# Weight sums moved from GpSimd to VectorE, and low halves of feed-forward weights formed by an accumulating DMA

## The chip, the cores and the metric

The kernel runs on one core of a Trainium2 chip. The time is device time of one launch in microseconds, the median of several runs. A profile is one execution, taken by the hardware profiler; its span runs from the first to the last instruction. In its rows PE is TensorE's matmul, PEld its weight load, DVE VectorE, ACT ScalarE, POOL GpSimd, and SP the engine that issues most DMAs. L12 is line 12 of the kernel.

## The reference

Two layers of an encoder for 512 positions of 1024 channels, in float32. Cut to what matters here:

```python
def reference(x, norm1_g, w_in, ..., w_out, norm2_g, w_ffn_in, w_ffn_out):
    for l in range(DEPTH):
        h = rmsnorm(x, norm1_g[l])
        ...    # differential attention, convolution branch, Fourier branch, gates
        x = x + merged @ w_out[l]
        h2 = rmsnorm(x, norm2_g[l])
        f_gate, f_up = jnp.split(h2 @ w_ffn_in[l], 2, axis=-1)
        x = x + (jax.nn.silu(f_gate) * f_up) @ w_ffn_out[l]
    return x
```

The feed-forward block is 2816 wide, which is 22 blocks of 128.

## The kernel before, in words

**Two halves of each number.** A float32 operand is used as a high half (a copy rounded to the float32r format, made on ScalarE) and a low half (the operand minus that copy, on VectorE). A product is then three matmuls: high by high, high by low and low by high. Everything is held with channels on the partitions and the 512 positions along the row.

**Weights in chunks.** The host lays all weights out as chunks of eight 128x128 blocks in the order of use. `chunk` loads one (512 KB, tile `raw`, shown as `wr`), lets ScalarE make `hi` (L201, tile `wh`) and VectorE `lo` (L202, tile `wl`). The pools hold WB = (3, 4, 4) buffers of `raw`, `hi` and `lo`. `gemm` uses the chunk block by block (L121).

**The feed-forward block.** It is done in two halves of eleven units; a half ends with eight outputs of the second projection (`gemm(act)`, L547 adds each to the residual), for which eleven chunks are loaded. A unit makes one block of the gate and one of the up projection in seven block products instead of eight (the scheme of Strassen and Winograd). `pair_weights` loads two chunks, `r1` with the blocks a21 and a11 and `r2` with a22 and a12, each 128x512, and forms

- s1 = a21 + a22 (L260), s3 = a11 - a21 written over a21 (L261), s2 = s1 - a11 (L263), s4 = a12 - s2 (L266), all on GpSimd;
- high and low halves of both loaded chunks, of which the first now holds s3 and a11 (L251 on ScalarE, L252 on VectorE, 128x1024 each);
- high and low halves of s1, s2 and s4 (L154 on ScalarE, L155 on VectorE, tiles `A` or `att`).

`combine` forms the matching sums of the input on VectorE (L295 to L298) while the attention output is being projected. `pair_gemm` runs the seven products (L281): four go into two banks of PSUM, then ScalarE copies the first bank (L328), VectorE adds the second (L329, tile `p15`), and TensorE adds three further products into the same banks, the last of them into the bank that L329 has read. `unit` then combines the banks on VectorE (L521 to L529), with a SiLU on ScalarE (L524), and splits the result for the second projection.

**What sets the order.** Nothing is in a hand-written order. Each instruction gets a priority, a due time that `self.t` counts up by the matmuls' lengths; the weights of a pair are asked for WLS = 20000 ns ahead, those of a chunk WL = 16000. A scheduler plays the program through with these priorities at build time and writes a fixed order for every engine; at run time each engine goes through its order and waits where an operand or a buffer isn't there yet. SP issues all weight loads, in order. GpSimd also adds squares for the norms (L353) and merges the branches (L574).

Of the kernel before, what the change touches and what calls it, by code (L numbers as in the profile page):

```python
# [9 lines left out]
F32 = mybir.dt.float32  # L10
F32R = mybir.dt.float32r
I32 = mybir.dt.int32  # L12
AF = mybir.ActivationFunctionType
ALU = mybir.AluOpType
AX = mybir.AxisListType

P = 128
L = 2
D = 1024
T = 512  # L20
# [9 lines left out]
CHUNK = 8  # L30
# [27 lines left out]
PEORD = False  # L58
CONV_LOW = -20000
WL = 16000  # L60
WB = (3, 4, 4)
WLS = 20000
HALF = 108
PASS = 216
MAGIC = 0x5F3759DF
# [23 lines left out]
class Hybrid:  # L89
# [102 lines left out]
    def chunk(self, l, c, t):  # L192
        nc = self.nc
        tc = self.tc
        keep = tc.cur_priority
        self.at(t - WL)
        raw = self.wp.tile([P, CHUNK * P], F32, tag="raw", name=self.nm("wr"), bufs=WB[0])
        nc.sync.dma_start(raw, self.a["w"][l, c])
        hi = self.wp.tile([P, CHUNK * P], F32R, tag="hi", name=self.nm("wh"), bufs=WB[1])
        lo = self.wp.tile([P, CHUNK * P], F32R, tag="lo", name=self.nm("wl"), bufs=WB[2])  # L200
        nc.scalar.copy(hi, raw)  # L201
        nc.vector.tensor_tensor(out=lo, in0=raw, in1=hi.bitcast(F32), op=ALU.subtract)  # L202
        tc.cur_priority = keep
        return hi, lo

# [23 lines left out]
    def pair_weights(self, early):  # L229
        nc, tc = self.nc, self.tc  # L230
        keep = tc.cur_priority
        self.at(self.t - WLS)
        raws = []
        for _ in range(2):
            raw = self.wp.tile([P, CHUNK * P], F32, tag="raw", name=self.nm("wr"), bufs=WB[0])
            c, k = divmod(self.wi, CHUNK)
            assert k == 0
            nc.sync.dma_start(raw, self.a["w"][self.l, c])
            self.wi += CHUNK
            raws.append(raw)  # L240
        r1, r2 = raws
        a21, a11 = r1[:, 0:T], r1[:, T : 2 * T]
        a22, a12 = r2[:, 0:T], r2[:, T : 2 * T]
        tags = ("qst", "kst", "ar") if early else ("cv", "cv", "cv")
        s1, s2, s4 = (self.slot(tag) for tag in tags)
        out = {}

        def halves(names, src):
            hi = self.wp.tile([P, CHUNK * P], F32R, tag="hi", name=self.nm("wh"), bufs=WB[1])
            lo = self.wp.tile([P, CHUNK * P], F32R, tag="lo", name=self.nm("wl"), bufs=WB[2])  # L250
            nc.scalar.copy(hi, src)  # L251
            nc.vector.tensor_tensor(out=lo, in0=src, in1=hi.bitcast(F32), op=ALU.subtract)  # L252
            for i, n in enumerate(names):
                out[n] = (hi[:, i * T : (i + 1) * T], lo[:, i * T : (i + 1) * T])

        def single(name, src):
            out[name] = self.split_to(src, "att" if early else "A")

        g = nc.gpsimd.tensor_tensor
        g(out=s1, in0=a21, in1=a22, op=ALU.add)  # L260
        g(out=a21, in0=a11, in1=a21, op=ALU.subtract)  # L261
        halves(("s3", "a11"), r1)
        g(out=s2, in0=s1, in1=a11, op=ALU.subtract)  # L263
        single("s1", s1)
        single("s2", s2)
        g(out=s4, in0=a12, in1=s2, op=ALU.subtract)  # L266
        halves(("a22", "a12"), r2)
        single("s4", s4)
        tc.cur_priority = keep
        return out  # L270

    def product(self, ps, w, xs, ks, start, stop):
        wh, wl = w
# [190 lines left out]
    def main(self, l):  # L464
        nc = self.nc
        sm = self.small
        hb = sm(24, "hb")
        nc.vector.tensor_scalar_mul(hb, self.par(l, "bg"), 0.5)
        hcw = sm(4 * CW, "hcw")
        nc.vector.tensor_scalar_mul(hcw, self.par(l, "cw"), 0.5)  # L470
        self.hb, self.hcw = hb, hcw
        self.glu(l)
        if l == 0:
            self.tables()
        self.qkv(l)
        self.heads(l, self.t + ATT0, ATT)
        self.four_c(l)
        merged = self.merged
        ths = []
        for m in range(KT):  # L480
            pg = self.gemm(self.h)
            ths.append(self.tanh(pg, 0, m, "A"))
        thb = [self.tanh(self.gemm(self.h), 1, m, "M") for m in range(LEAD_B)]
        self.drain("conv")
        for m in range(KT):
            py = self.gemm(self.cvs)
            self.merge(m, thb.pop(0), py)
            if m + LEAD_B < KT:
                thb.append(self.tanh(self.gemm(self.h), 1, m + LEAD_B, "M"))
        self.drain("att")  # L490
        ms = []
        for m in range(KT):
            py = self.gemm(self.atts)
            self.merge(m, ths[m], py)
            ms.append(self.split_to(merged[m], "cv" if m < 4 else "A"))
        x2, xc, acc = [None] * KT, [], None
        g2 = self.par(l, "g2")
        h = T // 2
        for q in range(KT // 2):
            us = self.wtp.tile([P, 2, T], F32, tag="wth", name=self.nm("us"))  # L500
            ts = self.wtp.tile([P, 2, T], F32, tag="wtl", name=self.nm("ts"))
            for i, m in enumerate((q, q + KT // 2)):
                xr = self.slot("M")
                self.at(self.t - 20000)
                getattr(nc, QS[3]).dma_start(xr, self.xin[m])
                self.at(self.t)
                ps = self.gemm(ms)
                xt = self.slot("V")
                nc.vector.scalar_tensor_tensor(out=xt, in0=ps, scalar=0.5, in1=xr, op0=ALU.mult, op1=ALU.add)
                nc.scalar.activation(us[:, i, :], xt, AF.Copy, scale=g2[:, m : m + 1])  # L510
                acc = self.sq_add(xt, acc, "M")
                x2[m] = xt
            xc.append(self.combine(us[:, 0, :], us[:, 1, :], (ts[:, 0, :], ts[:, 1, :]), XCT[q]))
        self.xg, self.acc = [], None
        xin = []
        rb2 = None

        def unit(j, b1, b2, qw):
            z = self.slot("M")
            v = nc.vector.tensor_tensor  # L520
            v(out=z[:, 0:h], in0=b1[:, 0:h], in1=rb2[:, 0:h], op=ALU.mult)  # L521
            v(out=z[:, h:T], in0=b1[:, h:T], in1=qw[:, 0:h], op=ALU.add)
            v(out=z[:, h:T], in0=z[:, h:T], in1=rb2[:, h:T], op=ALU.mult)  # L523
            nc.scalar.activation(z, z, AF.Silu)  # L524
            u = self.slot("M")
            v(out=u[:, 0:h], in0=b2[:, h:T], in1=qw[:, 0:h], op=ALU.add)
            v(out=u[:, h:T], in0=qw[:, 0:h], in1=qw[:, h:T], op=ALU.add)
            v(out=u, in0=u, in1=rb2, op=ALU.mult)
            v(out=u, in0=u, in1=z, op=ALU.mult)  # L529
            if j < 4:  # L530
                t = self.wtp.tile([P, 2, T], F32R, tag="wth" if j < 2 else "wtl", name=self.nm("act"))
                return self.split(u, t[:, 0, :], t[:, 1, :])
            if j < 7:
                return self.split_to(u, "qst", "kst")
            return self.split_to(u, "att")

        for half in range(2):
            act = []
            for j in range(NJ // 2):
                w = self.pair_weights(half == 0 and j < 4)  # L540
                got = self.pair_gemm(j, w, xc, half == 0 and j == 0)
                if half == 0 and j == 0:
                    rb2 = self.inv_rms(acc, D, "M", "rb")
                act.append(unit(j, *got))
            for m in range(KT):
                ps = self.gemm(act)
                nc.vector.tensor_tensor(out=x2[m], in0=ps, in1=x2[m], op=ALU.add)  # L547
                if half == 0:
                    continue
                if l == L - 1:  # L550
                    nc.sync.dma_start(self.out[m], x2[m])
                else:
                    sc = self.dram.tile([P, T], F32, tag=f"x{l}_{m}", name=f"x{l}_{m}")
                    getattr(nc, QS[3]).dma_start(sc, x2[m])
                    xin.append(sc)
                    self.next_x(l + 1, m, x2[m])
        self.xin = xin
        self.x = x2
# [630 lines left out]
```

## Time and profile before

| | |
|---|---|
| median of 3 runs | 1706.0 us (1704.88 to 1706.34) |
| profiled execution | 1702.3 us, span 1700.2 us |
| mean granted TensorE clock | 0.975 |
| TensorE matmul busy | 1625.8 us, 96% |
| VectorE busy | 1426.2 us, 84% |
| ScalarE busy | 791.7 us, 47% |
| GpSimd busy | 411.8 us, 24% |
| moved by DMA | 178.77 MB, mean 105 GB/s |

The halves of the feed-forward block lie, for the first layer, at about 460 to 655 and 655 to 855 us of the span, and for the second at about 1300 to 1500 and 1500 to 1700. In each, the units come first and the eight outputs of the second projection after them. A busy share of the whole span is an average over stages with different limits; the stages have to be read one by one.

### The profile page before, as it was taken

The page shows a single profiled execution, that of the slowest core. Times are in us where ns is not written, and L with a number is a line of the kernel's source. Part 1 is how long each engine was busy: PE and PEld are TensorE (multiplying, and loading weights), DVE is VectorE, ACT ScalarE, POOL GpSimd, SP SyncE. Part 2 cuts the span into 40 slices and gives each one's busy share as a digit, 9 for nine tenths or more (in the row PEclk, how much of TensorE's full clock was granted, in tenths as well). Part 3 has the DMA queues.
Part 4 walks back from the last instruction along what each step waited for, and adds up shares of the span by engine and source line. Part 5 has one row for each costly group of instructions (what it writes and reads, how often), then busy time and mean ns, then how long its engine had stood idle before and what let it go on. Part 6 is the DMA issues. An engine that isn't in the chain of part 4 may idle for free.

```text
span 1700.2 us, 24154 instructions
## 1 busy us (share of the span) xinstructions
PE 1625.8 (96%) x9096; PEld 1419.3 (83%) x9096; DVE 1426.2 (84%) x2220; ACT 791.7 (47%) x1267; POOL 411.8 (24%) x261
## 2 busy tenths in 40 slices
PE   8999999999987999889999999998999889998899
PEld 6888888887787988889888888886887889888897
DVE  7999999897999946997469999997779999379962
ACT  6445545753554423444343455557435544234430
POOL 3000000114455405551200000001145553065500
PEclk8999999999988999999999999999999899999999
DMA  5554234222422332223442532332234223332241
GB/s 198 167 162 143 75 101 125 81 84 82 129 76 87 100 100 87 88 87 106 137 136 88 186 121 90 105 102 68 79 98 123 74 87 100 99 93 82 87 124 50
DMA packets 61460, 178.77 MB, mean 105 GB/s; under 512 B 8976, under 2 KB 9872, under 8 KB 61344
## 3 DMA queue, kind: packets, MB, share of 16 engines
q1 hardware_dynamic: 60912, 176.11, 33.8%
q8 instruction: 71, 1.16, 0.3%
q0 software_dynamic: 432, 1.13, 0.3%
q14 instruction: 45, 0.37, 0.1%
HBM read 163.30 MB, written 13.89 MB: 104 GB/s over the span
## 4 chain that ended last, share of the span: by engine, by line
PE 75%; DVE 17%; issue 4%; ACT 2%; DMA 1%; POOL 1%; SPq 0%; DVEq 0%; POOLq 0%; ACTq 0%
PE main L121 51%; PE s L281 5%; PE att L281 4%; PE s L121 4%; PE att L121 3%; DVE M L529 3%; PE main L281 3%; DVE wl L252 3%; PE oth L121 3%; DVE A L155 3%; PE att L131 2%; DVE att L155 1%; DVE M L329 1%; DMA wr<-in_w 1%; DVE M L523 1%
## 5 line engine op out<-in xcount | busy, mean ns | idle before, releaser
L201 ACT CAST wh<-wr 128x1024 fp32r<-128x1024 f32 x180 | 188.9, 1051 | 281.3 <-PE main L121 153.1
L202 DVE TENSOR_TENSOR wl<-wr,wh 128x1024 fp32r<-128x1024 f32 x180 | 233.0, 1295 | 74.6 <-ACT wh L201 73.9
L121 PE MATMUL main<-X,wh 128*128 128x512 f32 x864 | 277.4, 395 | 0.0
L121 PEld LDWEIGHTS main<-X,wh 128*128 128x128 f32 x864 | 161.4, 189 | 32.8 <-issue 0.5
L988 DVE SCALAR_TENSOR_TENSOR cv<-cv,hcw,cv 128x497 f32<-128x497 f32 (+14 forms) x240 | 176.6, 736 | 1.2
L121 PE MATMUL main<-X,wl 128*128 128x512 f32 x432 | 170.9, 396 | 0.0
L251 ACT CAST wh<-wr 128x1024 fp32r<-128x1024 f32 x88 | 92.4, 1050 | 116.5 <-PE att L281 29.4
L252 DVE TENSOR_TENSOR wl<-wr,wh 128x1024 fp32r<-128x1024 f32 x88 | 141.2, 1605 | 5.5 <-ACT wh L251 5.4
L1019 POOL TENSOR_TENSOR cv<-cv,cv 128x512 f32<-128x512 f32 x6 | 9.8, 1630 | 515.6 <-DVE cv L988 515.6
L260 POOL TENSOR_TENSOR cv<-wr,wr 128x512 f32<-128x512 f32 x36 | 53.4, 1485 | 298.0 <-DMA wr<-in_w 254.9
L121 PE MATMUL main<-att,wh 128*128 128x512 f32 x384 | 119.4, 390 | 1.5 <-ACT att L154 1.5
L155 DVE TENSOR_TENSOR A<-cv,A 128x512 fp32r<-128x512 f32 x108 | 108.7, 1008 | 13.2 <-ACT A L154 12.9
L812 ACT ACTIVATE at<-s,mx 128x512 f32<-128x512 f32 x128 | 88.1, 689 | 58.3 <-DVE mx L810 51.8
L121 PE MATMUL main<-A,wh 128*128 128x512 f32 x320 | 106.4, 391 | 0.0
L121 PE MATMUL main<-wh,X 128*128 128x512 f32 x288 | 96.7, 391 | 0.0
L154 ACT CAST A<-cv 128x512 fp32r<-128x512 f32 x108 | 65.4, 617 | 65.8 <-PE s L281 22.9
L121 PEld LDWEIGHTS main<-X,wl 128*128 128x128 f32 x432 | 81.6, 189 | 17.1 <-issue 0.5
L810 DVE TENSOR_REDUCE mx<-s 128x1 f32<-128x512 f32 x128 | 86.7, 681 | 3.8 <-PE s L121 3.1
L547 DVE TENSOR_TENSOR V<-main,V 128x512 f32<-128x512 f32 x32 | 22.1, 690 | 77.5 <-PE main L121 77.5
L121 PEld LDWEIGHTS main<-att,wh 128*128 128x128 f32 x384 | 71.8, 188 | 17.2 <-ACT att L154 1.7
L121 PE MATMUL main<-cv,wh 128*128 128x512 f32 x240 | 78.4, 395 | 2.9 <-ACT cv L154 2.8
L121 PE MATMUL main<-act,wh 128*128 128x512 f32 x256 | 80.2, 394 | 0.0
(324 smaller groups left out, 4399.2 us busy)
## 6 DMA issues: line engine op xcount, KB each, us to landing
wr<-in_w SPq DMA_DIRECT2D x268, 512.0 KB, 3.6
dqk<-at SPq DMA_DIRECT2D x32, 256.0 KB, 3.7
qst<-dqk SPq DMA_DIRECT2D x96, 64.0 KB, 1.9
kst<-dqk SPq DMA_DIRECT2D x96, 64.0 KB, 1.9
V<-in_xT SPq DMA_DIRECT2D x8, 256.0 KB, 7.0
att<-dftd SPq DMA_DIRECT2D x8, 256.0 KB, 4.5
M<-in_xT SPq DMA_DIRECT2D x8, 256.0 KB, 3.5
x<-V SPq DMA_DIRECT2D x8, 256.0 KB, 2.6
```

The lines of the kernel that those rows point to most:

```text
L121: return self.pin(self.nc.tensor.matmul(out, lhsT=lhsT, rhs=rhs, start=start, stop=stop))
L154: self.lasthi = nc.scalar.copy(hi, src)
L155: nc.vector.tensor_tensor(out=lo, in0=src, in1=hi.bitcast(F32), op=ALU.subtract)
L201: nc.scalar.copy(hi, raw)
L202: nc.vector.tensor_tensor(out=lo, in0=raw, in1=hi.bitcast(F32), op=ALU.subtract)
L251: nc.scalar.copy(hi, src)
L252: nc.vector.tensor_tensor(out=lo, in0=src, in1=hi.bitcast(F32), op=ALU.subtract)
L260: g(out=s1, in0=a21, in1=a22, op=ALU.add)
L281: self.nc.tensor.matmul(ps, lhsT=a[:, s], rhs=b, start=start and k == ks[0] and i == 0, stop=last and i == 2, skip_group_check=True,)
L810: nc.vector.tensor_reduce(out=mx, in_=ps, axis=AX.X, op=ALU.max, negate=True)
L812: nc.scalar.activation(e, ps, AF.Exp, bias=mx, accum_out=z1 if c else z0)
L988: ins = nc.vector.scalar_tensor_tensor(out=acc[:, a:b], in0=g[:, a + d : b + d], scalar=w[:, t : t + 1], in1=acc[:, a:b], op0=ALU.mult, op ...
```

## The change

- The four sums of a pair are instructions of VectorE and not of GpSimd.
- For weights that go into the products as they were loaded (a11, a22, a12, and all of the second projection) VectorE no longer subtracts. ScalarE writes the negated operand, rounded, into `lo` (`low_by_dma`), and GpSimd issues a DMA that reads the same weights from HBM a second time and adds them to what lies in `lo`. For s3, which isn't in HBM, VectorE still subtracts, on 128x512.
- The switch `by_dma` is set from the feed-forward block's start to the end of the layer; the chunks of all other projections are split as before.
- The buffers of `raw`, `hi` and `lo` are (3, 3, 5), and a pair's weights are asked for 26000 ns ahead.

```diff
-WB = (3, 4, 4)
-WLS = 20000
+WB = (3, 3, 5)
+WLS = 26000
...
         hi = self.wp.tile([P, CHUNK * P], F32R, tag="hi", name=self.nm("wh"), bufs=WB[1])
         lo = self.wp.tile([P, CHUNK * P], F32R, tag="lo", name=self.nm("wl"), bufs=WB[2])
+        if self.by_dma:
+            self.low_by_dma(lo, raw, self.a["w"][l, c])
         nc.scalar.copy(hi, raw)
-        nc.vector.tensor_tensor(out=lo, in0=raw, in1=hi.bitcast(F32), op=ALU.subtract)
+        if not self.by_dma:
+            nc.vector.tensor_tensor(out=lo, in0=raw, in1=hi.bitcast(F32), op=ALU.subtract)
...
-        g = nc.gpsimd.tensor_tensor
-        g(out=s1, in0=a21, in1=a22, op=ALU.add)
-        g(out=a21, in0=a11, in1=a21, op=ALU.subtract)
-        halves(("s3", "a11"), r1)
-        g(out=s2, in0=s1, in1=a11, op=ALU.subtract)
-        single("s1", s1)
-        single("s2", s2)
-        g(out=s4, in0=a12, in1=s2, op=ALU.subtract)
-        halves(("a22", "a12"), r2)
-        single("s4", s4)
+        c = self.wi // CHUNK - 2
+        self.low_by_dma(l1[:, T : 2 * T], a11, self.a["w"][self.l, c][:, T : 2 * T])
+        self.low_by_dma(l2, r2, self.a["w"][self.l, c + 1])
+        g = nc.vector.tensor_tensor
+        g(out=s1, in0=a21, in1=a22, op=ALU.add)
+        g(out=a21, in0=a11, in1=a21, op=ALU.subtract)
+        nc.scalar.copy(h1, r1)
+        g(out=l1[:, 0:T], in0=a21, in1=h1[:, 0:T].bitcast(F32), op=ALU.subtract)
+        g(out=s2, in0=s1, in1=a11, op=ALU.subtract)
+        for name, src in (("s1", s1), ("s2", s2)):
+            out[name] = self.split_to(src, "att" if early else "A")
+        nc.scalar.copy(h2, r2)
+        g(out=s4, in0=a12, in1=s2, op=ALU.subtract)
+        out["s4"] = self.split_to(s4, "att" if early else "A")
...
+    def low_by_dma(self, lo, raw, src):
+        self.nc.scalar.activation(lo, raw, AF.Copy, scale=-1.0)
+        self.nc.gpsimd.dma_start(lo, src, accum_op=ALU.add)
```

The scheduler then writes other orders. In what follows a row is an engine's instruction with its line, operation, output, inputs and shape; the lines of the changed kernel are seven to nine higher (L329 is L336, L529 is L537). VectorE before, from one sum L329 of a unit in the second half, first layer, to the end of that unit's block L529 (`wr` the loaded chunk, `cv` a sum of weights, `M` the unit's tiles):

```order
L329 TENSOR_TENSOR M_7404<-s_7355,M_7404 128x512
L155 TENSOR_TENSOR kst_7320<-M_7314,qst_7319 128x512
L155 TENSOR_TENSOR A_7485<-cv_7463,A_7484 128x512
L521 TENSOR_TENSOR M_7443<-s_7354,rb_4821 128x256
L522 TENSOR_TENSOR M_7443<-s_7354,M_7404 128x256
L527 TENSOR_TENSOR M_7448<-M_7404 128x256
L155 TENSOR_TENSOR A_7606<-cv_7595,A_7605 128x512
L523 TENSOR_TENSOR M_7443<-M_7443,rb_4821 128x256
L526 TENSOR_TENSOR M_7448<-s_7355,M_7404 128x256
L528 TENSOR_TENSOR M_7448<-M_7448,rb_4821 128x512
L252 TENSOR_TENSOR wl_7615<-wr_7593,wh_7614 128x1024
L529 TENSOR_TENSOR M_7448<-M_7448,M_7443 128x512
```

One more L155 and one more L252 follow before the next L329: 14 instructions a unit. VectorE after, from the same place one unit earlier:

```order
L336 TENSOR_TENSOR M_7332<-main_7283,M_7332 128x512
L155 TENSOR_TENSOR A_7416<-cv_7391,A_7415 128x512
L155 TENSOR_TENSOR kst_7245<-M_7239,qst_7244 128x512
L259 TENSOR_TENSOR cv_7526<-wr_7522,wr_7524 128x512
L260 TENSOR_TENSOR wr_7522<-wr_7522 128x512
L263 TENSOR_TENSOR cv_7527<-cv_7526,wr_7522 128x512
L529 TENSOR_TENSOR M_7371<-main_7282,rb_4824 128x256
L530 TENSOR_TENSOR M_7371<-main_7282,M_7332 128x256
L535 TENSOR_TENSOR M_7376<-M_7332 128x256
L155 TENSOR_TENSOR A_7543<-cv_7526,A_7542 128x512
L267 TENSOR_TENSOR cv_7528<-wr_7524,cv_7527 128x512
L534 TENSOR_TENSOR M_7376<-main_7283,M_7332 128x256
```

L531, L262 (the low half of s3), L536, L155 and L537 follow: 17 instructions a unit, none of them wider than 512. The sums stand between L336 and the unit's own work.

GpSimd after, from the last unit of that half into the second projection. Before, the four sums of each unit stood here, and nothing for the second projection but the sums of squares (L353, now L360):

```order
L277 DMA wlo_7941<-in_w 128x512
L277 DMA wlo_7943<-in_w 128x1024
L277 DMA wl_8074<-in_w 128x1024
L277 DMA wl_8105<-in_w 128x1024
L277 DMA wl_8146<-in_w 128x1024
L277 DMA wl_8188<-in_w 128x1024
L277 DMA wl_8219<-in_w 128x1024
L277 DMA wl_8261<-in_w 128x1024
L277 DMA wl_8303<-in_w 128x1024
L360 TENSOR_TENSOR M_8175<-M_8125,M_8175 128x512
L277 DMA wl_8345<-in_w 128x1024
```

Each unit has an accumulating DMA of 128x512 and one of 128x1024 now, and the second projection one for each chunk, with the sums of squares between the last of them.

ScalarE after, around the copy L335 (before: L328) of the same unit; L261 and L266 are the high halves of the two chunks, L276 the negated copies:

```order
L266 CAST whi_7257<-wr_7250 128x1024
L154 CAST A_7278<-cv_7254 128x512
L154 CAST act_7108<-M_7103 128x512
L276 ACTIVATE wlo_7395<-wr_7387 128x1024
L154 CAST A_7405<-cv_7389 128x512
L261 CAST whi_7392<-wr_7385 128x1024
L276 ACTIVATE wlo_7530<-wr_7522 128x512
L154 CAST A_7409<-cv_7390 128x512
L335 COPY M_7332<-main_7282 128x512
```

The negated copies of the next unit and of the one after it stand ahead of the copy that L336 waits for.

More of the change, by code (lines that the diff above doesn't have):

```diff
@@ L246, in pair_weights @@
         out = {}
[L248 to L252, printed above, removed]
+        h1, l1, h2, l2 = (
+            self.wp.tile([P, CHUNK * P], F32R, tag=tag, name=self.nm("w" + tag), bufs=WB[i])
+            for tag, i in (("hi", 1), ("lo", 2), ("hi", 1), ("lo", 2))
+        )
+        c = self.wi // CHUNK - 2
[12 more added lines that the diff above has]
+        out["s4"] = self.split_to(s4, "att" if early else "A")
+        for names, hi, lo in ((("s3", "a11"), h1, l1), (("a22", "a12"), h2, l2)):
             for i, n in enumerate(names):
                 out[n] = (hi[:, i * T : (i + 1) * T], lo[:, i * T : (i + 1) * T])
-        def single(name, src):
-            out[name] = self.split_to(src, "att" if early else "A")
-        g = nc.gpsimd.tensor_tensor
-        g(out=s1, in0=a21, in1=a22, op=ALU.add)
-        g(out=a21, in0=a11, in1=a21, op=ALU.subtract)
-        halves(("s3", "a11"), r1)
-        g(out=s2, in0=s1, in1=a11, op=ALU.subtract)
-        single("s1", s1)
-        single("s2", s2)
-        g(out=s4, in0=a12, in1=s2, op=ALU.subtract)
-        halves(("a22", "a12"), r2)
-        single("s4", s4)
         tc.cur_priority = keep
         return out
+    def low_by_dma(self, lo, raw, src):
+        self.nc.scalar.activation(lo, raw, AF.Copy, scale=-1.0)
+        self.nc.gpsimd.dma_start(lo, src, accum_op=ALU.add)
     def product(self, ps, w, xs, ks, start, stop):
@@ L471, in main @@
         self.hb, self.hcw = hb, hcw
+        self.by_dma = False
         self.glu(l)
@@ L535, in unit @@
             return self.split_to(u, "att")
+        self.by_dma = True
         for half in range(2):
```

## The prediction

> **What bounds the kernel now.** I read the page's busy times first, then the stretches of the feed-forward products, then one unit on VectorE, GpSimd and TensorE in order of time, and last the waits of TensorE.
>
> The page gives TensorE 96% of the span, so the whole gain must come from the missing 4% and from time in which TensorE is slowed. Per stage (columns: stretch, its length, busy time and instructions of each engine, granted clock, DMA share, GB/s) the first four rows run from the first to the last sum L329 of a half of the feed-forward block, the fifth lies in the output projection of that block, the last two are the beginnings of the first halves:
>
> ```profile
> 483.10:601.00 117.90, 106.51 (x823) 105.01 (x823) 112.82 (x141) 57.12 (x82) 54.11 (x32) 0.94 0.30 88
> 672.20:789.40 117.20, 106.78 (x836) 105.08 (x835) 114.80 (x140) 52.89 (x77) 55.28 (x33) 0.96 0.29 88
> 1326.80:1444.00 117.20, 106.44 (x823) 104.53 (x822) 113.37 (x142) 57.09 (x82) 53.34 (x32) 0.94 0.30 88
> 1515.20:1632.30 117.10, 106.69 (x836) 104.98 (x834) 114.69 (x139) 52.79 (x77) 55.98 (x33) 0.96 0.30 88
> ...
> 611.00:661.00 50.00, 50.00 (x220) 40.90 (x219) 21.51 (x22) 12.11 (x14) 10.56 (x7) 1.00 0.32 102
> ...
> 455.00:483.10 28.10, 21.00 (x107) 17.85 (x106) 26.38 (x25) 12.50 (x21) 16.69 (x12) 0.84 0.30 91
> 1297.00:1326.80 29.80, 23.60 (x117) 19.85 (x116) 28.56 (x28) 14.68 (x24) 17.95 (x12) 0.84 0.30 89
> ```
>
> VectorE (third pair) is busy 113 to 115 of 117 us in the product stages, TensorE only 106 to 107, at a clock of 0.94 to 0.96. Ten units take 117.3 us on average. One unit on VectorE, from one L329 to the next, has no gap:
>
> ```profile
> 709.86 0.68 DVE L329 TENSOR_TENSOR M<-s,M 128x512 f32<-128x512 f32 x1
> 710.46 0.68 DVE L155 TENSOR_TENSOR act<-M,act 128x512 fp32r<-128x512 f32 x1
> ...
> 711.66 0.41 DVE L521 TENSOR_TENSOR M<-s,rb 128x256 f32<-128x256 f32 x1
> 711.99 0.41 DVE L522 TENSOR_TENSOR M<-s,M 128x256 f32<-128x256 f32 x1
> ...
> 714.04 1.56 DVE L528 TENSOR_TENSOR M<-M,rb 128x512 f32<-128x512 f32 x1
> 715.52 2.31 DVE L252 TENSOR_TENSOR wl<-wr,wh 128x1024 fp32r<-128x1024 f32 x1
> 717.76 1.77 DVE L529 TENSOR_TENSOR M<-M,M 128x512 f32<-128x512 f32 x1
> 719.45 1.78 DVE L155 TENSOR_TENSOR A<-cv,A 128x512 fp32r<-128x512 f32 x1
> 721.15 1.21 DVE L252 TENSOR_TENSOR wl<-wr,wh 128x1024 fp32r<-128x1024 f32 x1
> 722.29 0.68 DVE L329 TENSOR_TENSOR M<-att,M 128x512 f32<-128x512 f32 x1
> ```
>
> The unit lasts 12.43 us. From 714.04 to 721.15 the same operations take 1.6 to 1.8 us that take 0.68 before and after; L252 takes 2.31 and then 1.21. That is when GpSimd forms its four sums:
>
> ```profile
> 713.75 1.30 POOL L260 TENSOR_TENSOR cv<-wr,wr 128x512 f32<-128x512 f32 x1 [5.50 <-DVE M L523]
> 715.13 1.62 POOL L261 TENSOR_TENSOR wr<-wr 128x512 f32<-128x512 f32 x1
> 716.71 2.27 POOL L263 TENSOR_TENSOR cv<-cv,wr 128x512 f32<-128x512 f32 x1
> 719.07 1.62 POOL L266 TENSOR_TENSOR cv<-wr,cv 128x512 f32<-128x512 f32 x1
> ```
>
> TensorE pays for it at the matmul that may overwrite the bank which L329 reads, and again afterwards:
>
> ```profile
> 704.13 1.24 PE L281 MATMUL s<-X,A 128*128 128x256 f32 x9
> 705.21 0.52 PE L281 MATMUL s<-B,A 128*128 128x256 f32 x3
> ...
> 723.02 0.79 PE L281 MATMUL att<-X,wh 128*128 128x256 f32 x2 [2.10 <-DVE M L329]
> 723.61 0.41 PE L281 MATMUL att<-X,wl 128*128 128x256 f32 x1
> 723.82 0.63 PE L281 MATMUL att<-X,wh 128*128 128x256 f32 x2
> ```
>
> Undisturbed, nine matmuls take 1.08 us, 0.120 each; after a wait two take 0.59 us before the next can start, then one 0.21. The waits in total (us, times, longest):
>
> ```profile
> PE att L281 <- DVE M L329: 15.7, 10, 2.1
> PE main L281 <- DVE M L329: 15.4, 10, 4.1
> PE s L281 <- DVE B L155: 5.8, 2, 2.9
> PE s L281 <- DVE M L329: 5.6, 4, 2.0
> ...
> PE s L281 <- ACT M L328: 4.3, 2, 2.1
> ```
>
> So the product stages are set by VectorE's ring of work, through L329, and everything else by TensorE.
>
> **VectorE.** A unit loses both L252 (2.31 and 1.21) and keeps its other 12 instructions; it gains four sums of 128x512 and one low half of 128x512. Start to start, an undisturbed 512-wide operation takes 0.60 us (709.86 to 710.46) and a 256-wide one 0.33 (711.66 to 711.99). After the change a unit has 17: twelve of 512 and five of 256, 12 x 0.60 + 5 x 0.33 = 8.9 us, if nothing on GpSimd disturbs them.
>
> Now the bound on that. GpSimd still issues two DMAs a unit. The nearest row is the issue of a plain one:
>
> ```profile
> L454 POOL DMA_DIRECT2D at<-in_dft x3 | 1.6, 546 | 38.3 <-DMA dftd<-at 38.3
> ```
>
> If each 0.55 us stopped VectorE altogether, a unit would be 10.0 us; if not at all, 8.9. I take 8.9: the long rows above coincide with sums, not with issues. The Trainium skill's page "SBUF — State Buffer", section "Who interferes with whom", says that two-input VectorE work collides with GpSimd work that reads SBUF, not with work that only writes it. By that rule descriptor writing costs VectorE nothing and 8.9 stands; the 2.31 against 1.21 agrees with its first half, and no run here shows the second.
>
> **TensorE.** A unit is 7 products x 4 blocks x 3 matmuls = 84, at 0.120 us 10.1 us. That is over 8.9 and over the pessimistic 10.0, so TensorE becomes the bound. The four product stretches hold 823 + 836 + 823 + 836 = 3318 matmuls: 398.2 us instead of 469.4. That is the main term, **-71.2 us**: about half waiting, half slowed matmuls.
>
> **The beginnings.** The last two rows of the first fence lose 7.1 and 6.2 us idle at a clock of 0.84, behind sums of the input that GpSimd also stretches (first row untouched, second beside a sum):
>
> ```profile
> 471.96 0.41 DVE L296 TENSOR_TENSOR ts<-us 128x256 f32<-128x256 f32 x1
> 472.30 1.48 DVE L297 TENSOR_TENSOR ts<-us,ts 128x256 f32<-128x256 f32 x1
> ```
>
> VectorE takes on sums of three units there, 3 x 5 x 0.60 = 9 us against 6.8 saved (six L252 at 1.14 step), and loses the stretching. Between 0 and 13 us in all; I take **-8**, since the chain from the last output block through the splits remains.
>
> **ScalarE.** It gains a negated copy of 512 and one of 1024 per unit, and one of 1024 per output chunk. Nearest rows:
>
> ```profile
> L251 ACT CAST wh<-wr 128x1024 fp32r<-128x1024 f32 x88 | 92.4, 1050 | 116.5 <-PE att L281 29.4
> L154 ACT CAST A<-cv 128x512 fp32r<-128x512 f32 x108 | 65.4, 617 | 65.8 <-PE s L281 22.9
> ```
>
> 52.9 us in ten units is 5.3 each; with 1.05 + 0.62 it is 7.0 of 10.1. It stays below, but these copies wait in order for a load and for a free buffer, with the L328 copy behind them; between that copy and the matmul that needs it lie 30 matmuls, 3.6 us. Nothing, or as much as 0.5 us a unit (22 us) if the cover fails; I take 0.3 for each of the 44 units, **+13**, some three times the 4.3 us of L328 waits quoted above.
>
> **DMA.** Added are 0.75 MB per unit and 0.5 MB per output chunk, read again from HBM and added to what lies in SBUF. The trace shows no accumulating transfer. A plain load keeps the engines at a share of 0.32 for 102 GB/s (fifth row): 0.524 MB cost 1.64 us of all sixteen.
>
> ```profile
> wr<-in_w SPq DMA_DIRECT2D x268, 512.0 KB, 3.6
> ...
> at<-in_dft POOLq DMA_DIRECT2D x2, 256.0 KB, 3.2
> ```
>
> From below: as much as a load, 1.64. From above: two transfers of the GpSimd queue in series with nothing overlapped, 6.4 us. A chunk of the output projection lasts 24 matmuls x 50/220 us = 5.45 us, so accumulating must stay under 5.45 - 1.64 = 3.8 us, 2.3 loads. In a unit the limit is (10.1 - 3.3) / 1.5 = 4.5 us. I take two loads, 3.3 us, because each byte needs two fetches and one write: 91% of the engines in the projection, 82% in the products. It then costs nothing on the path. The Trainium skill, "Collectives: The Full Stack", section "The bandwidth ceiling: the fold count and why AG ≠ RS ≠ AR", blames the half rate of a reducing transfer on two source reads, not on the addition. By that rule the price is 3.3 and the sum is unchanged; no run here shows it yet. Lateness is covered: the low halves' five buffers let a transfer start about a unit before its matmul, 10 us against 3.6.
>
> **Buffers of the other stages.** High halves have three buffers, not four. The copy is now released 16 us before its use (three chunks) and then 10.9. It needs 1.05 for the copy and, by
>
> ```profile
> L202 DVE TENSOR_TENSOR wl<-wr,wh 128x1024 fp32r<-128x1024 f32 x180 | 233.0, 1295 | 74.6 <-ACT wh L201 73.9
> ```
>
> 1.3 for the low half. 8 us are left for queues, so I put 0; without that cover it is rival (c). The weights of a pair are asked for 26 and not 20 us ahead in the scheduler's time, but with three raw buffers as before SP still waits for a buffer and gains nothing from it; 0.
>
> **GpSimd's queue.** An accumulate waits there for ScalarE's negated copy, and behind it stand the sums of squares (L360) of the attention output's projection and of the last output projection. A square on ScalarE waits for such a sum. In ScalarE's own order the negated copies stand ahead of those squares too, so a square that runs has the accumulate ahead of its sum already released; what is left is the issue, 0.55 us, five times a layer, beside VectorE's longer chain there: 0, or 3 us a layer at most.
>
> **Sum.** 1702.3 (profiled execution, span 1700.2) - 71.2 - 8 + 13 = 1636. The median lies 3.7 above that execution: **1640**.
>
> **The rivals.**
> (a) *The DMA engines become the bound.* It decides from 2.3 loads per accumulate in the projection. For it: 91% leaves little, and nothing shows the price. Against: two fetches are only 3.3 us. At 3.4 loads (5.6 us) a chunk takes 7.2 us, 44 x 1.8 = +79, and a unit 3.3 + 8.4 = 11.7, as now: 1706 + 79 = **1785**. At 6.4 it is some 1870; at 3 the gain is just used up.
> (b) *A new wait replaces L329*: ScalarE held up by loads, or low halves late. For it: ScalarE's queue before L328 grows; against: 3.6 us of cover. Half the main term: **1676**.
> (c) *Three high buffers starve the other stages.* For it: 180 chunks depend on it; against: 8 us of cover. Half a microsecond per chunk, +90: **1730**.
>
> **How the numbers follow.** Forecast 0.60, own range 1615 to 1665; (a) 0.19, (b) 0.14, (c) 0.07. A difference under 0.2% (3.4 us) can't be told from none here. Faster: 0.60 + 0.14 + 0.02 from (a) between 2.3 and 3 loads = 0.76; same 0.03; slower 0.21. The low end, 1612, is both gains whole and no ScalarE loss (1627) less some more relief at the beginnings. The high end, 1735, takes in (b), (c) and the mild part of (a), and leaves some 0.13 above.
>
> **What would show it.** Right: L336 (now L329) every 10.1 to 10.5 us, VectorE with gaps and no 1.7 us operations, clock near 1.00 in the product stages. Wrong: TensorE waiting for DMA on wlo or wl and a DMA share near 1 in the projection (a); waits on ScalarE's L335 (b); waits on L203 or L205 outside the feed-forward block (c).

## The result and the profile after

The changed kernel takes **1650.95 us** (median of 4, 1647.29 to 1655.13) against 1705.44 for the kernel before: ratio 0.9685, 95% interval 0.9657 to 0.9714, some 54 us less. The prediction was 1640. Its profiled execution took 1652.3 us, with a span of 1650.5.

The page of the changed kernel, first its busy times, then its DMA queues (packets, MB, share of the sixteen engines), then its transfers with the median time to landing:

```profile
PE 1601.2 (97%) x9096; PEld 1397.1 (85%) x9096; DVE 1247.5 (76%) x2308; ACT 889.0 (54%) x1399; POOL 229.3 (14%) x217
...
q1 hardware_dynamic: 60912, 176.11, 33.4%
q0 software_dynamic: 19440, 58.81, 21.2%
...
wr<-in_w SPq DMA_DIRECT2D x268, 512.0 KB, 4.4
wlo<-in_w POOLq DMA_DIRECT2D x44, 512.0 KB, 5.6
wl<-in_w POOLq DMA_DIRECT2D x44, 512.0 KB, 7.3
```

VectorE fell from 84% to 76%, ScalarE is at 54%. The accumulating transfers (queue q0) hold the engines for 21% of the span, and a plain load of a chunk now lands after 4.4 us, where it was 3.6.

The stretches that the prediction used, in the changed kernel (columns as there): the four product stretches from first to last sum L336 (before: L329), a piece of the output projection, and the beginning of each first half:

```profile
481.00:586.10 105.10, 99.83 (x805) 97.42 (x804) 84.21 (x162) 67.46 (x100) 17.29 (x20) 1.00 0.72 167
660.00:760.90 100.90, 97.85 (x806) 97.05 (x807) 83.89 (x160) 64.20 (x95) 16.71 (x20) 1.00 0.72 169
1296.20:1406.50 110.30, 102.17 (x804) 99.75 (x803) 84.37 (x162) 67.31 (x100) 17.32 (x20) 0.97 0.68 160
1477.90:1582.90 105.00, 100.59 (x823) 99.19 (x823) 83.94 (x160) 64.77 (x95) 16.76 (x20) 1.00 0.70 163
...
601.00:626.00 25.00, 25.00 (x111) 20.49 (x110) 2.77 (x4) 10.43 (x11) 4.91 (x6) 1.00 0.99 228
...
455.00:481.00 26.00, 22.73 (x128) 19.78 (x127) 19.45 (x30) 14.94 (x24) 6.88 (x6) 0.87 0.61 146
1268.00:1296.20 28.20, 24.74 (x145) 21.83 (x144) 22.42 (x35) 16.77 (x26) 7.29 (x7) 0.94 0.64 154
```

The four stretches add up to 421.3 us, 48.1 less than the 469.4 before; the two spans differ by 49.7. The first sum starts at 481.0 instead of 483.1, and from the last sum of the first layer to the first of the second it is 535.3 us instead of 537.4: 2.1 us less each. VectorE is busy 84 of 101 to 110 us. TensorE still loses time: its 3238 matmuls there would take 388.6 us at 0.120, so 32.7 us are lost (before: 469.4 - 398.2 = 71.2). The loss fell by 38.5; the other 9.6 us of the 48.1 are the 80 matmuls that the new order puts outside these stretches. Of them 44 lie ahead of the two first sums (2275 matmuls up to 481.0 where 2257 lay up to 483.1, and 2555 against 2529 in the 535.3 us). That is 5.3 us of work, so the beginnings gained 4.2 + 5.3 = 9.5 us by work done.

One unit on VectorE in the changed kernel, in order of time:

```profile
689.55 0.69 DVE L336 TENSOR_TENSOR M<-s,M 128x512 f32<-128x512 f32 x1
...
692.40 0.69 DVE L259 TENSOR_TENSOR cv<-wr,wr 128x512 f32<-128x512 f32 x1 [0.97 <-DMA wr<-in_w]
...
693.74 0.69 DVE L263 TENSOR_TENSOR cv<-cv,wr 128x512 f32<-128x512 f32 x1
...
699.61 0.68 DVE L336 TENSOR_TENSOR M<-att,M 128x512 f32<-128x512 f32 x1
```

No operation is stretched, the unit lasts 10.06 us, and VectorE now has a gap: it waits for a load. GpSimd in order of time, in the same unit: its issue at 693.81 lies beside the sum of 693.74 and leaves it at 0.69.

```profile
693.81 0.87 POOL L277 DMA_DIRECT2D wlo<-in_w  x1 [7.17 <-ACT wlo L276]
```

What TensorE waits for in the feed-forward block, and what ScalarE's negated copies L276 wait for (us in total, times, longest):

```profile
PE s L288 <- ACT whi L261: 8.5, 7, 3.6
...
PE main L288 <- ACT M L335: 2.8, 5, 1.1
PE main L288 <- ACT whi L261: 2.2, 2, 1.3
PE att L288 <- ACT M L335: 2.1, 2, 1.2
PE att L288 <- ACT whi L261: 1.9, 3, 1.0
...
ACT wlo L276 <- DMA wr<-in_w: 120.4, 37, 5.4
...
ACT wl L276 <- DMA wr<-in_w: 78.7, 35, 4.6
```

The waits for L329 (36.7 us in the three rows of before) are nearly gone. In their place stands ScalarE: 12.6 us for high halves (L261) and 4.9 us for L335. ScalarE itself stands 199 us at negated copies whose raw chunk has not landed, with the high halves and L335 behind them in its order.

### The profile page after: what moved, and what is told of

Read it like the earlier page. It is cut to its first block, busy times and chain, and to the rows that moved or that the text cites. A ratio compares the mean times of both kernels' runs of the same rounds, so it can differ in the third digit from the quotient of the medians.

```text
span 1650.5 us, 24460 instructions
## 1 busy us (share of the span) xinstructions
PE 1601.2 (97%) x9096; PEld 1397.1 (85%) x9096; DVE 1247.5 (76%) x2308; ACT 889.0 (54%) x1399; POOL 229.3 (14%) x217
## 4 chain that ended last, share of the span: by engine, by line
PE 72%; DMA 11%; DVE 11%; ACT 3%; issue 2%; SPq 0%; DVEq 0%; ACTq 0%
PE main L121 53%; DMA wr<-in_w 11%; PE s L121 4%; PE att L121 3%; PE oth L121 3%; PE att L288 3%; PE s L288 3%; PE att L131 2%; PE main L288 1%; DVE wr L260 1%; DVE cv L259 1%; DVE wlo L262 1%; DVE A L155 1%; DVE cv L263 1%; DVE cv L267 1%
## 5 line engine op out<-in xcount | busy, mean ns | idle before, releaser
L203 ACT CAST wh<-wr 128x1024 fp32r<-128x1024 f32 x180 | 188.5, 1049 | 210.7 <-PE main L121 103.4
L205 DVE TENSOR_TENSOR wl<-wr,wh 128x1024 fp32r<-128x1024 f32 x136 | 178.6, 1313 | 28.9 <-ACT wh L203 28.0
L276 ACT ACTIVATE wlo<-wr 128x512 fp32r<-128x512 f32 x88 | 74.0, 844 | 125.5 <-DMA wr<-in_w 120.4
L277 POOL DMA_DIRECT2D wlo<-in_w x88 | 76.5, 869 | 413.6 <-ACT wlo L276 286.5
L276 ACT ACTIVATE wl<-wr 128x1024 fp32r<-128x1024 f32 x44 | 46.6, 1059 | 80.5 <-DMA wr<-in_w 78.7
L259 DVE TENSOR_TENSOR cv<-wr,wr 128x512 f32<-128x512 f32 x36 | 25.0, 693 | 82.3 <-DMA wr<-in_w 82.3
L155 DVE TENSOR_TENSOR A<-cv,A 128x512 fp32r<-128x512 f32 x108 | 73.7, 684 | 3.6 <-ACT A L154 3.6
```

Of the source, the lines that this page charges most:

```text
L276: self.nc.scalar.activation(lo, raw, AF.Copy, scale=-1.0)
L277: self.nc.gpsimd.dma_start(lo, src, accum_op=ALU.add)
```

## Experiments

Ratios are to the kernel before on the same chip, with their 95% interval; where kernels of different chips are compared, it is by these ratios, 0.001 being 1.7 us.

### The sums alone

The question is whether VectorE's ring only has to lose its collision with GpSimd, or must also lose its low halves.

```diff
-        g = nc.gpsimd.tensor_tensor
+        g = nc.vector.tensor_tensor
```

> The four sums of a pair on VectorE, everything else as before the change (low halves by VectorE, buffers 3, 4, 4, weights asked for 20000 ns ahead). Theory: the gain came from VectorE's ring of work per unit, which must fit under TensorE's 10.1 us. Here a unit has seven operations of 512 (4.2 us), five of 256 (1.7), two of 1024 (2.3) and four sums (2.4): 10.6 us, so VectorE still sets the pace by a little, 10.6 to 10.8 us between the sums, and the time is 1655 to 1668. Rival: all of the gain is the end of the collisions with GpSimd, and the accumulating DMA only takes something back: 1640 to 1652. Second rival: the DMA part carries the gain: 1680 or more.

Measured: **1622.86 us**, ratio 0.9527 (0.9513 to 0.9541). One word gives some 80 us, 27 more than the whole change. This kernel's four product stretches, by the same columns, and the last 26 us before 481:

```profile
474.60:579.80 105.20, 102.72 (x828) 100.65 (x827) 101.72 (x173) 56.94 (x82) 0.00 (x0) 1.00 0.32 101
646.40:749.80 103.40, 102.81 (x844) 101.97 (x844) 99.02 (x169) 51.54 (x76) 0.00 (x0) 1.00 0.35 104
1277.70:1382.70 105.00, 102.66 (x828) 100.61 (x827) 101.78 (x173) 56.67 (x82) 0.00 (x0) 1.00 0.32 101
1449.20:1555.00 105.80, 105.26 (x857) 104.14 (x857) 99.84 (x171) 52.29 (x77) 0.00 (x0) 1.00 0.34 105
...
455.00:481.00 26.00, 25.04 (x171) 22.60 (x170) 24.39 (x37) 16.95 (x26) 4.89 (x3) 1.00 0.32 94
```

One low half on VectorE in it, in order of time:

```profile
685.19 1.23 DVE L252 TENSOR_TENSOR wl<-wr,wh 128x1024 fp32r<-128x1024 f32 x1
```

VectorE is busy 94 to 97% of these stretches, and that is enough: L252 is at 1.23 us, not 2.31, and TensorE loses 419.4 - 3357 x 0.120 = 16.6 us instead of 71.2. The beginnings are better too: the first sum starts at 474.6 (8.5 us earlier than before), and from 749.8 to 1277.7 it is 527.9 us (9.5 less). So most of the gain needs no relief of VectorE from its low halves; what the relief is worth beyond that, a later run shows. The time is below all three expectations. A unit takes 10.5 us on average (419.4 / 40), about the 10.6 that was expected, so the miss lies in the rest of the kernel: it took 1230.8 us before and takes 1199.3 here, some 5 of the 31.5 us because 39 more matmuls lie in the stretches.

### The accumulating DMA alone

```diff
-        g = nc.vector.tensor_tensor
+        g = nc.gpsimd.tensor_tensor
...
-        g(out=l1[:, 0:T], in0=a21, in1=h1[:, 0:T].bitcast(F32), op=ALU.subtract)
+        nc.vector.tensor_tensor(out=l1[:, 0:T], in0=a21, in1=h1[:, 0:T].bitcast(F32), op=ALU.subtract)
```

(against the changed kernel: the sums go back to GpSimd)

> The changed kernel with the four sums on GpSimd again. Theory: VectorE's own work is 8.9 - 2.4 = 6.5 us a unit, but during GpSimd's 6.8 us of sums it gets through only some four operations at 1.7 us instead of 0.6, which makes 10.9 us: 1660 to 1675, VectorE operations of 1.7 us again, and the accumulating DMAs issued late behind the sums in GpSimd's queue. Rival (the sums' place carries everything): near before, 1690 to 1705. Rival (the subtractions carry everything): 1651.

Measured: 1724.6 us, ratio 1.0130 (1.0111 to 1.0149): by itself this half, which in this run includes the new buffers and lead, makes the kernel slower by 1.3%, which none of the three expectations allowed for. A product stretch of this kernel, by the same columns:

```profile
670.10:795.60 125.50, 109.76 (x845) 107.76 (x844) 91.96 (x126) 67.27 (x97) 64.19 (x56) 0.95 0.68 151
```

One operation of VectorE there, with the idle time ahead of it:

```profile
701.97 1.68 DVE L155 TENSOR_TENSOR A<-cv,A 128x512 fp32r<-128x512 f32 x1 [2.98 <-ACT A L154]
```

GpSimd at that time:

```profile
700.44 1.29 POOL L259 TENSOR_TENSOR cv<-wr,wr 128x512 f32<-128x512 f32 x1 [5.83 <-DMA wr<-in_w]
701.81 1.29 POOL L260 TENSOR_TENSOR wr<-wr 128x512 f32<-128x512 f32 x1
```

VectorE has time to spare here (92 of 125.5 us), and the stretch is longer than the 117.2 before. Beside a sum its operation still takes 1.68 us. The longest waits of TensorE show the rest:

```profile
PE att L288 <- ACT M L335: 16.4, 8, 3.2
PE s L288 <- ACT M L335: 12.5, 10, 3.2
PE main L288 <- ACT M L335: 12.5, 7, 2.7
```

41 us go to L335, ScalarE's copy behind the negated copies. By these two runs the halves are -80 (with the buffers of before) and +22 (with those of the change), and together they gave -54.

### Buffers and lead

The change also set the weight buffers (raw, high, low) from 3, 4, 4 to 3, 3, 5 and the lead from 20000 to 26000. Three runs take the changed kernel with both back, the lead back, the buffers back:

```diff
-WB = (3, 3, 5)
+WB = (3, 4, 4)
...
-WLS = 26000
+WLS = 20000
```

> The changed kernel with the buffers (3, 4, 4) and 20000 ns of before. Theory: neither sets the pace; the low halves' fourth buffer comes free 4 to 5 us before it must be filled, so 1648 to 1662. Rival: the fifth low buffer covers the accumulating transfers' 4.5 to 7.3 us; without it TensorE waits for low halves in every unit and in the second projection: 1670 or more. Rival (c) of the prediction, that three high buffers starve the other stages: those stages gain here, 1640 or less.

> The changed kernel with the pairs' lead of 20000 ns alone, buffers 3, 3, 5 kept. The changed kernel with both put back came to 1630.6, 20 us less. Theory: three high buffers do the harm, since the high copy of a pair's first chunk can be made only when the previous pair's second chunk is used up, and the loads behind it come late (TensorE waits for L261 in the changed kernel, not with four): this run stays at 1645 to 1655, with the waits for L261. Rival: the lead does it, because ScalarE's order puts negated copies ahead of their loads: 1628 to 1636 and no waits of L276 for loads.

> The changed kernel with the buffers 3, 4, 4 alone, the lead of 26000 ns kept. Theory (three high buffers do the harm): 1628 to 1636, no waits for L261. Rival (the lead does it): 1645 to 1655, with L276 waiting for loads.

Measured: both back 1630.64 us, 0.9578 (0.9563 to 0.9594); lead alone 1646.86, 0.9658 (0.9640 to 0.9676), not told apart from the change; buffers alone 1634.14, 0.9585 (0.9562 to 0.9608). The lead does nothing at all: in the traces, with either lead, every engine goes through the same instructions in the same order (by line, operation, operands and names without their numbers), with the new buffers and with the old. So these are two orders, each timed twice, and the buffers cost 17 us (0.9685 against 0.9585) or 14 (0.9658 against 0.9578). TensorE's waits for low halves in the kernel with both back:

```profile
PE main L121 <- DMA wl<-in_w: 3.1, 3, 2.0
...
PE main L288 <- DMA wlo<-in_w: 2.8, 2, 1.6
...
PE att L288 <- DMA wlo<-in_w: 1.9, 2, 1.0
```

And its transfers, with the median time to landing:

```profile
wr<-in_w SPq DMA_DIRECT2D x268, 512.0 KB, 4.1
wlo<-in_w POOLq DMA_DIRECT2D x44, 512.0 KB, 7.8
wl<-in_w POOLq DMA_DIRECT2D x44, 512.0 KB, 8.3
```

The negated copies' waits for loads, 199 us in the changed kernel, are not among this kernel's waits, nor are TensorE's for L261. What TensorE waits for now is the accumulated low halves themselves, which land after 7.8 and 8.3 us: 7.8 us in all. The kernel stays 8.7 us behind the sums alone (0.9578 against 0.9527), though its four product stretches (402.9 us, 3259 matmuls) lose less than theirs, 11.8 against 16.6 us. So what it loses lies outside them; how much of that is these waits isn't shown.

The same buffers and lead without any accumulating transfer (the sums alone, with 3, 3, 5 and 26000):

```diff
-WB = (3, 4, 4)
+WB = (3, 3, 5)
...
-WLS = 20000
+WLS = 26000
```

> The sums on VectorE alone, as in the run of 1622.9, but with the buffers 3, 3, 5 and the lead of 26000 ns of the change, without any accumulating DMA. Theory: the buffers and the lead harm by the order of ScalarE's copies and not by the transfers: 1635 to 1650. Rival: they only harm together with the accumulating transfers, which make the loads late: 1620 to 1628.

Measured: 1627.63 us, 0.9542 (0.9528 to 0.9557), which overlaps with the sums alone. So the three high and five low buffers are seen to be dear only together with the transfers. Which of the two numbers matters was not tried; they were changed together.

### Which transfers

The output projection's low halves back on VectorE, the units' low halves still by DMA; first with the buffers of the change, then with the old buffers and lead:

```diff
-        self.by_dma = True
+        self.by_dma = False
```

> The changed kernel with the low halves of the second projection by VectorE again, the pairs unchanged. Theory: the projection is paced by TensorE either way; the DMA share there falls from 0.98 to about 0.33, VectorE rises from 3 to about 9 of 25 us, and the time moves only by the start of the next half, where loads now wait for accumulates: 1643 to 1651. Rival: the saturated DMA engines delay the pairs that follow by more, 1640 or less. Second rival: VectorE's subtractions come late at the change of stage, 1655 or more.

> The changed kernel with the buffers 3, 4, 4 and the lead of 20000 ns, and the projection's low halves on VectorE, so that only the pairs' are accumulated. Theory: it saves the 7 us that this gave with the buffers 3, 3, 5, from 1630.6: 1620 to 1626, level with the sums alone (1622.9). Rival: with four high buffers the projection's accumulates cost nothing: 1629 to 1634.

Measured: 1643.65 us, 0.9654 (0.9628 to 0.9680), and 1628.55 us, 0.9561 (0.9545 to 0.9577). Neither can be told from its partner with the projection's transfers (0.9685 and 0.9578); the second lies between its two expectations. The projection, where the engines are at a share of 0.99, is not where most of the time goes: it is worth some 5 and 3 us by these ratios, within their intervals.

### The price of the transfer

In the changed kernel the accumulating transfers are left out, and then replaced by plain copies of the same bytes:

```diff
         self.nc.scalar.activation(lo, raw, AF.Copy, scale=-1.0)
-        self.nc.gpsimd.dma_start(lo, src, accum_op=ALU.add)
```

> The changed kernel without the accumulating DMAs: the low half is the negated rounded operand alone, the addition is left out, so the output is not the reference's; ScalarE's negated copies, buffers and lead stay. Theory: the transfers themselves cost little, since TensorE waits mainly for ScalarE's copies L261 and L335: 1640 to 1650. Rival: the transfers make the loads late (4.4 to 6.6 us to landing and not 3.6), and ScalarE's copies wait for those: 1622 to 1632, without L276 waiting for loads.

```diff
-        self.nc.gpsimd.dma_start(lo, src, accum_op=ALU.add)
+        self.nc.gpsimd.dma_start(lo, src)
```

> The changed kernel with a plain copy from HBM in place of each accumulate, on the same queue and of the same size; the low half is then the whole operand, so the addition is left out. In the changed kernel an accumulate of 0.5 MB takes 3.06 us of all sixteen engines in the projection and a load 1.59. Theory (the second fetch is the price): a plain copy takes about 1.6 us, the DMA share in the projection falls from 0.98 to 0.6 to 0.65, loads land in about 4 us, and the time is 1620 to 1635, most of the way to the 1612.8 without transfers. Rival (any DMA from GpSimd's queue costs this much, by its descriptors): share 0.9 or more, 1643 to 1655.

Measured: 1612.76 us, 0.9451 (0.9434 to 0.9468) without them, and 1617.96 us, 0.9495 (0.9476 to 0.9514) with plain copies. Both are below the lowest that was expected. A product stretch without the transfers:

```profile
645.40:744.80 99.40, 99.40 (x830) 99.36 (x829) 85.08 (x161) 66.41 (x96) 0.00 (x0) 1.00 0.35 104
```

ScalarE's waits for loads in the same kernel:

```profile
ACT wlo L276 <- DMA wr<-in_w: 52.6, 32, 3.5
...
ACT wl L276 <- DMA wr<-in_w: 6.0, 10, 1.4
```

TensorE is busy for the whole stretch, 0.120 us a matmul. The negated copies are still there; their waits for loads fall from 199 to 59 us. With 3, 3, 5 and 26000 throughout, the steps are: sums on VectorE 0.9542, low halves taken off VectorE 0.9451 (-16 us), their bytes fetched a second time 0.9495 (+8), and added rather than copied 0.9685 (+32). The first two steps also change the engines' orders. The last does not: the traces of the kernel with plain copies and of the changed kernel have the same instructions in the same order on every engine, so these 32 us come from the transfer and its issue alone.

How late the raw loads land in the first product stretch, in the changed kernel (481.0 to 586.1), with plain copies (476.8 to 574.5) and with the buffers and lead of before (474.8 to 577.4):

```profile
wr<-in_w SPq DMA_DIRECT2D x20, 512.0 KB, 5.4
...
wr<-in_w SPq DMA_DIRECT2D x21, 512.0 KB, 4.3
...
wr<-in_w SPq DMA_DIRECT2D x20, 512.0 KB, 5.2
```

Beside accumulating transfers a load lands 1.1 us later than beside copies. With the old buffers it lands nearly as late as in the changed kernel, but there no negated copy waits for a load, and the product stretches lose 11.8 us instead of 32.7. Of these two kernels, late loads were dear only in the one where ScalarE stood in its order waiting for them.

Why adding is dearer than copying is in the DMA queues, here over 20 us of the output projection of the changed kernel (604 to 624):

```profile
q0 software_dynamic: 611, 2.24, 65.4%
q1 hardware_dynamic: 586, 2.11, 32.0%
...
wl<-in_w POOLq DMA_DIRECT2D x4, 512.0 KB, 7.3
wr<-in_w SPq DMA_DIRECT2D x4, 512.0 KB, 6.6
```

The same queues with plain copies (590 to 610):

```profile
q1 hardware_dynamic: 564, 2.09, 35.0%
q0 software_dynamic: 472, 1.68, 29.1%
```

A chunk is 0.524 MB. Accumulated it took 65.4% of 20 us for 2.24 / 0.524 = 4.27 chunks, **3.06 us** of all sixteen engines; loaded, 6.4 / 4.03 = **1.59 us**: a ratio of 1.93. A plain copy took 5.8 / 3.21 = 1.82, about a load (beside it 7.0 / 3.99 = 1.75). And raw chunks land after 6.6 us beside accumulating transfers.

Last, the projection's accumulating transfers doubled:

```diff
             self.low_by_dma(lo, raw, self.a["w"][l, c])
+            nc.gpsimd.dma_start(lo, self.a["w"][l, c], accum_op=ALU.add)
```

> The changed kernel with a second accumulate of the same weights for each chunk of the second projection, so that the low half there holds one operand too much; the pairs are unchanged. It doubles the suspected load where the DMA engines were at 0.98. Theory (the engines' time is the bound there, a load 1.59 us and an accumulate 3.06): a chunk needs 1.59 + 2 x 3.06 = 7.7 us and not TensorE's 5.4, which is 44 x 2.3 = 100 us more: 1735 to 1765, TensorE waiting for the low halves in the projection. Rival (a share of 0.98 only counts queued packets and there is room): 1651 to 1680.

Measured: 1753.73 us, 1.0292 (1.0271 to 1.0313), 103 us above the change. A piece of the projection, by the same columns:

```profile
610.00:630.00 20.00, 15.18 (x54) 11.93 (x55) 0.69 (x1) 3.99 (x4) 3.54 (x4) 0.83 1.00 201
```

TensorE's longest wait in that kernel:

```profile
PE main L121 <- DMA wl<-in_w: 74.2, 23, 8.1
```

At 1.59 + 2 x 3.06 = 7.7 us of transfers per chunk against TensorE's 5.45, the 44 chunks should cost 44 x 2.3 = 99 us, and they cost 103. The engines are full in this piece (share 1.00) and TensorE waits; the change, with one transfer a chunk, stays below that. One rival is left: GpSimd issues a chunk's second transfer only when the first has landed, after 7.7 us by the median in this piece, so a chain of landings would give a like price.

## Why the prediction came out as it did

**The ring.** Right. VectorE set the product stages because GpSimd's sums stretched it, and without them TensorE sets them. VectorE's 17 operations were put at 8.9 us; from 689.55 to 699.61 they take 10.06 less the gap of 0.97, 9.1. GpSimd's issue takes 0.87 us, not 0.55, and stretches nothing, as taken; the upper bound of 10.0 did not come up. On average a unit takes 10.1 to 11.0 us in the four stretches, so only one of them comes down to TensorE's 10.1. The clock is 1.00 in three of the four stretches and 0.97 in one. The Trainium skill, "SBUF — State Buffer", section "Who interferes with whom", has it that GpSimd work which only writes SBUF does not collide with two-input work of VectorE; if issuing a DMA is such work, the trace agrees, 0.69 us beside an issue and 1.68 beside a sum.

**The main term, -71.2.** In the changed kernel 38.5 of it came. With the sums alone it is 54.6, and in the stretch shown without the transfers TensorE loses nothing at all. The term was right in cause; what was set against it was too small.

**The beginnings, -8.** By work done -9.5 in the changed kernel, and with the sums alone 8.5 + 9.5 and 18 more matmuls ahead of the two first sums (2.2 us), -20. That the term is near 8 in the changed kernel is luck: the gain was underestimated, and the other half of the change took some 10 of it back.

**ScalarE, +13, and DMA, 0.** Here a step failed. Two loads per accumulate was right (1.93), and so was that the engines do not become the bound. The Trainium skill, "Collectives: The Full Stack", section "The bandwidth ceiling: the fold count and why AG ≠ RS ≠ AR", puts the half rate of a reducing transfer down to two source reads; the trace agrees with the price, 3.06 against 1.59 us, and does not show the reads. The projection's share of 0.99 instead of 0.91 comes from transfers running ahead: 4.27 chunks in 20 us where TensorE uses 20 / 5.45 = 3.7. But **"It then costs nothing on the path"** was wrong by 40 us (0.9451 to 0.9685) with the buffers of the change; with those of before the kernel is still 22 us above the one without transfers (0.9578). The lateness checked was that of the accumulated half; what came late was the other traffic, the raw loads (3.6 to 4.4 us, 5.4 in the first product stretch, 6.6 in the projection), and everything in ScalarE's order behind a negated copy that waits for one. The +13 was meant for that order, but priced as if loads kept their time: the negated copies as such cost nothing that shows, since the kernel that keeps them without the transfers is 16 us faster than the sums alone with the same buffers, and in the stretch shown TensorE loses nothing.

**Buffers, 0.** Right for the other stages: between the two layers' feed-forward stretches the time did not grow (535.3 against 537.4). With the sums alone it is 529.8 us with 3, 3, 5 and 527.9 with 3, 4, 4, and 17 more matmuls (2.0 us) lie in the first. Wrong within the feed-forward block, which the step did not look at: with the transfers, 3, 3, 5 costs 14 to 17 us against 3, 4, 4. That it acts through the order of ScalarE is what the waits and the landing times of the two kernels suggest; a run that changes this order alone was not made. That the lead gives nothing was right: it changes no order.

**GpSimd's queue, 0.** Right as far as the runs show: taking the projection's transfers out of that queue changed nothing that can be told (0.9654 and 0.9561 against 0.9685 and 0.9578).

**The sum.** Gains of 79.2 and a cost of 13 were added up. Measured with the buffers of the change, the gains are 94 (0.9451) and the cost 40. A cost that was 27 us too low met a gain that was 14 too low, and the median came out 11 above the forecast. That it came so near is luck: with the cost alone off, it would have been some 1667, outside the forecast's own range.

**The rivals.** (a) did not happen, and its threshold isn't contradicted: 1.93 is under 2.3 loads, and with twice the transfers the projection's engines are full and TensorE waits. (b) happened in part, through L261 (12.6 us) more than through L335 (4.9). (c) did not happen where it was placed. Not among them was that one half of the change loses: the sums alone beat both kernels.

## What to carry to other kernels

Where a change has two halves, time each: here one word was worth 80 us, and the other half with its buffers cost some 27 of them. A transfer whose engine time fits can still cost, by making other loads late for an engine that takes its work in order, so price the loads beside it, and look at what stands behind them in that order. Before relieving an engine that is full, look for what stretches its operations.

## What the runs showed of the hardware

An accumulating DMA from HBM into SBUF held the sixteen engines 1.93 times as long as a load of the same bytes, and its issue took GpSimd 0.87 us where a plain copy's took 0.53:

```profile
602.84 0.53 POOL L277 DMA_DIRECT2D wl<-in_w  x1 [4.97 <-ACT wl L276]
```

(the kernel with plain copies, GpSimd in order of time). A share of the DMA engines near 1 does not by itself say that TensorE waits for them: it was 0.99 in the projection of the changed kernel, where TensorE was busy for all 25 us, and 1.00 with the transfers doubled, where it was busy 15.18 of 20 us. Operations of VectorE on 128x512 took 1.56 to 1.78 us beside GpSimd's sums and 0.68 without. A sum of GpSimd took 1.29 us beside such an operation (701.81, in the kernel with the DMA alone) and 1.29 with VectorE waiting (700.44), but up to 2.27 in the kernel before; whether GpSimd loses too is not settled.
